# Chunk attention scores with 128 contraction rows, first weights in quarters, and a longer schedule search in a two-layer hybrid encoder

## The chip, the cores and the metric

The kernel runs on one core of a Trainium2 chip. The metric is the device time of one execution in microseconds; several executions give a median. A profiled execution also gives a trace of every instruction of the core's engines: TensorE (PE; its weight loads are shown apart as PEld), VectorE (DVE), ScalarE (ACT), GpSimd (POOL), and SyncE (SP), which here only issues DMAs.

## What is computed

The input is x of 512 tokens by 1024 channels, all in float32. Each of two layers applies an RMS norm and one input projection, whose columns feed three groups of attention heads; the heads' outputs are normalised, concatenated and projected back into x. Then come a second norm and a gated feed-forward part with a causal convolution of width 3. A last norm closes the program. Cut to its outline:

```python
for l in range(2):
    proj = rms_norm(x, attn_norm[l]) @ w_in[l]
    h_mla, h_diff, h_ch = split(proj)
    o_mla  = rms_norm(mla_attention(h_mla, ...))      # 6 heads, latent q and kv, rotary key
    o_diff = diff_attention(h_diff, ...)              # 6 heads, two softmaxes each
    o_ch   = rms_norm(chunk_attention(h_ch, bias))    # 4 heads of 64, the scores of this change
    x = x + concat(o_mla, o_diff, o_ch) @ w_out[l]
    x = x + conv_ffn(rms_norm(x, ffn_norm[l]), ...)   # silu(g) * u, width 2816
return rms_norm(x, final_norm)
# chunk attention, per head: softmax(q @ k.T / 8 + bias[clip(i - j)]) @ v,
# chunks of 64 tokens, causal by chunk
```

## The kernel before

**Tiles and precision.** Activations lie transposed: 128 channels on the partitions, 512 tokens along the free axis. So x is eight tiles of 128x512. A weight block is 128x128 and the moving operand 128x512. TensorE multiplies fp32r numbers, which keep only the upper part of an fp32 number. To keep precision every operand is split in two: hi, the number cast to fp32r, and lo, what is left (`split`, L581: a cast on ACT or DVE, then a subtraction on DVE, called a low here). A product is three matmuls into one PSUM bank, hi·hi, hi·lo and lo·hi (`mm3` L576, `proj` L768). A projection of 1024 channels to 128 columns is thus 24 matmuls of 512 columns, and nearly all of TensorE's time is such matmuls.

**Weights.** They stream in once, 512 KB for a unit of 128 columns, through SP's queue (`weights`, L539). `halves` (L555) makes their hi and lo; for most the lo is a negated hi to which a DMA of POOL's queue adds the raw weights. The first three units (kv, q0, q1 of layer 0) come in two half DMAs each, cast and subtracted on DVE, while x lands in eight DMAs (`load_inputs`, L610).

**Stages of a layer.** `ORDER` (L81) lists the units: latent projections (kv, q0, q1, kr), the values (v, e, g), expansions of the latents (u), q and k of the differential heads (d) and of the chunk heads (c), and the output weights (a, b). A unit waits for its weights, for a PSUM bank (three for projections, two for scores, two for transposes and sums, one for products) and for its gate. Beside the units run two streams: `scores` (L1270) goes through the heads in the order latent, differential, chunk, each in four blocks of 128, 256, 384 and 512 keys (`softmax_rows`, L787: matmuls, then a reduction on DVE, then an exponential on ACT); `products` (L1294) transposes the probabilities and multiplies them with the values. Scores of the latent heads contract 128 rows, and those of the differential heads 96, which `stack` (L1092) gathers by DMAs of POOL's queue.

**Chunk heads.** `chunk_qk` (L936) makes two units, q and k of two heads at once: a tile of 128 partitions holds head 2u in rows 0 to 63 and head 2u+1 in rows 64 to 127, each with hi and lo. `chunk_head` (L1069) takes one head's 64 rows, and `three` (L808) gives three matmuls a block:

```python
return [(qt[r0 : r0 + n, a, :], kt[r0 : r0 + n, b, :]) for a, b in ((0, 0), (0, 1), (1, 0))]
```

**Latent values.** `latent_values` (L1015) projects the normalised latent to values in four blocks of 384 columns; DVE evicts each from its PSUM bank with the normalisation as factor.

**Second norm.** Each time an output projection is added to a tile of x, `gain_f.add` splits the tile for the feed-forward part and adds its square to a running sum; in `run_b` (L1144) that add runs on POOL.

**The order of instructions.** Every call of an engine is recorded (`Engine.call`, L357) with an estimated cost and its dependences, not issued; so in the trace nearly all instructions carry the line L364. When the whole program is recorded, `Clock.emit` (L335) orders it by a list schedule, backward and forward in turn, `ROUNDS` (L76) times, and keeps the one whose last start is earliest. Then everything is issued in that order, so the order on each engine is fixed ahead of the run and an instruction waits for all before it on its engine.

Of the kernel before, what the change touches and what calls it, by code (L numbers as in the profile page):

```python
# [52 lines left out]
for u in range(2):  # L53
    RINGS_R[f"cq{u}"], RINGS_R[f"ck{u}"] = ([RINGS_R["kmla"][2 * u + n]] for n in range(2))
    RINGS_R[f"vc{u}"] = [v[1 + u]]
for n in range(6):
# [3 lines left out]
for t, w, n in (("wraw", 1024, 2), ("P", GCOLS, 2), ("P1", GCOLS, 1), ("ev", S, 2), ("rb", S, 1), ("me", S, 1), ("acc", S, 1),  # L60
                ("y", S, 1), ("s", S, 1), ("o", S, 6), ("ol", S, 1)):
    RINGS_F[t] = (w, list(range(NF, NF + w * n, w)))
    NF += w * n
p0, o0, ol0 = (RINGS_F[t][1] for t in ("P", "o", "ol"))
RINGS_F["oc"], RINGS_F["om"], RINGS_F["od"] = (S, o0[0:2]), (S, o0[0:3]), (S, o0[3:6])
RINGS_F["ol"], RINGS_F["rbias"] = (S, [o0[5], ol0[0], o0[4]]), (S, [o0[2], ol0[0]])
# [8 lines left out]
NEVER = 1e9  # L75
ROUNDS = 4  # L76
TABLES = {AF.Exp: 1, AF.Ln: 1, AF.Sin: 2, AF.Silu: 3}
OUT = (1, 4, 7)
LATE = dict(qk=0, qm=0.5, og=0, lat=0, po=-99, hp=0, hs=99, sc=-0.2, p1=-0.5, st=-1, w=4)

ORDER = "kv q0 q1 kr e0 v e1 u0 u1 u2 d0 d1 d2 e2 c0 c1 g0 g1 a0 a1 a2 a3 a4 a5 a6 a7 b0 b1"  # L81

# [6 lines left out]
OA_FROM = 6  # L89
AHEAD = 1  # L90
NB_OUT = 1 << (8 // KB).bit_length() - 1

# [28 lines left out]
class Clock:  # L121
# [213 lines left out]
    def emit(self):  # L335


        start = self.list_schedule(list(range(len(self.ops))), lambda o: o.needs, lambda o: o.users, True)
        best = start
        for _ in range(ROUNDS):  # L340
            back = self.list_schedule([-(start[o.n] + o.cost) for o in self.ops], lambda o: o.users, lambda o: o.needs, False)
            start = self.list_schedule([-(back[o.n] + o.cost) for o in self.ops], lambda o: o.needs, lambda o: o.users, True)
            best = min(best, start, key=max)
        for o in sorted(self.ops, key=lambda o: (best[o.n], o.n)):
            o.emit()
# [134 lines left out]
def encoder(ctx, tc, xT, pos_row, pos_col, wflat, small, lam, relx, cst, out):  # L480
# [58 lines left out]
    def weights(l, name, run, finish, gate=lambda: True):  # L539
        o, c = offs[l, name]  # L540
        runs = [(0, c // 2), (c // 2, c)] if l == 0 and len(work.jobs) < 3 else [(0, c)]

        def part(raw, a, b):
            sp.dma_start(raw[:, a:b], wflat[o : o + P * c].rearrange("(p c) -> p c", p=P)[:, a:b])

        def fetch():
            raw = T("wraw")
            part(raw, *runs[0])
            if work.jobs[0].raw is None:
                rest_of_first.append(lambda: part(raw, *runs[1]))  # L550
            elif len(runs) > 1:
                part(raw, *runs[1])
            return raw
# [27 lines left out]
    def split(src, hi, lo):  # L581
# [6 lines left out]
        dve.tensor_tensor(lo, src, hi.bitcast(F32), op=ALU.subtract)  # L588


    widths = [KD * S, GCOLS, S, L * NCOL, cst.shape[1], P, NB, NB, 1]
# [18 lines left out]
    def load_inputs():  # L610

        work.jobs[0].fetch()
        sp.dma_start(sm[0], small[0])
        for k in range(KD):
            sp.dma_start(xs[k], xT[:, k, :])
            if k == 0:
                rest_of_first.pop()()
            if k == 1:
                work.jobs[1].fetch()
        sp.dma_start(posk_i, bass.AP(tensor=pos_row.tensor, offset=0, ap=[[0, P], [1, S]]))  # L620
        sp.dma_start(ct, cst)
        sp.dma_start(posq_i, pos_col)
# [185 lines left out]
    def three(qt, kt, r0, n):  # L808

        return [(qt[r0 : r0 + n, a, :], kt[r0 : r0 + n, b, :]) for a, b in ((0, 0), (0, 1), (1, 0))]  # L810
# [72 lines left out]
    def layer(l, gain_a):  # L883
# [51 lines left out]

        def chunk_qk(u):  # L936
            gate = lambda: (1, 1, 1) in stacks if u else ("m", 2, 1) in scored
            return [qk_unit(f"cq_{u}", f"cq{u}", gate, imm=CH_SCALE), qk_unit(f"ck_{u}", f"ck{u}", gate)]

# [129 lines left out]
        def chunk_head(h, qt, kt, buf, res):  # L1069
            rbias = biases[h]  # L1070
            yield from softmax_rows(three(qt, kt, 64 * (h % 2), 64), lambda i: rbias[:, S - 128 * (i + 1) :], -1.0, res, buf)
            scaled(*res)
            if h + 2 < CH_H:
                biases.append(load_bias(h + 2))
# [69 lines left out]
        def run_b(t, w):  # L1144
            for n in range(NB_OUT):
                c = slice(128 * KB * n, 128 * KB * (n + 1))
                acc = yield from proj(og[KA:], (w[0][:, c], w[1][:, c]), [])
                add_to_x(NB_OUT * t + n, acc)
                gain_f.add(NB_OUT * t + n, pool)

        jobs = {}

        def job(name):
            kind, t = name[0], int(name[1:]) if name[1:].isdigit() else 0
            return {
                "c": lambda: chunk_qk(t),
                "d": lambda: diff_qk(t),
# [93 lines left out]
        if l == 0:  # L1251
            load_inputs()
            exp_tables()
            work.jobs[0].load()
            for k in range(KD):
                gain_a.split(k)
                if k in (1, 4):
                    work.jobs[1 + k // 4].load()
            gain_a.squares()
            setup_rope()  # L1260
# [9 lines left out]
        def scores():  # L1270
            for n, (kind, u, j) in enumerate(heads):

                over = max((k + 1 for k in range(n) if bufs[k] in bufs[n] + "X" * (kind == "d")), default=0)
                need = [jobs[f"u{u}"]] if kind == "m" else jobs[f"{kind}{u}"][:2]
                yield lambda: 0.0 if all(b.done for b in need) and (kind != "d" or (u, j, 0) in stacks) and tailed[0] >= over else NEVER
# [251 lines left out]
```

## Time and profile before

| | before |
|---|---|
| device time, 3 runs | 1240.38, 1240.6, 1242.81 us; median 1240.6 |
| profiled execution | 1241.23 us, its span 1239.1 us |
| granted TensorE clock, mean | 0.995 |
| PE, PEld, DVE, ACT, POOL busy | 98%, 80%, 69%, 57%, 10% |
| moved by DMA | 146.33 MB, mean 118 GB/s |

Busy time is a share of the span, over stages that differ. The program's stages lie in time as follows: the start to about 15 us; the attention of layer 0 to about 240; its output projection and feed-forward part to about 640; then the same for layer 1, and the last norm at the end. A timeline lists instructions by start; consecutive like ones are one row with their count, and a bracket at the end gives the engine's idle time just before and what ended it. Ends of matmuls are modelled; their starts are recorded.

### The profile page before, as it was taken

The page shows a single profiled execution, that of the slowest core. Times are in us where ns is not written, and L with a number is a line of the kernel's source. Part 1 is how long each engine was busy: PE and PEld are TensorE (multiplying, and loading weights), DVE is VectorE, ACT ScalarE, POOL GpSimd, SP SyncE. Part 2 cuts the span into 40 slices and gives each one's busy share as a digit, 9 for nine tenths or more (in the row PEclk, how much of TensorE's full clock was granted, in tenths as well). Part 3 has the DMA queues.
Part 4 walks back from the last instruction along what each step waited for, and adds up shares of the span by engine and source line. Part 5 has one row for each costly group of instructions (what it writes and reads, how often), then busy time and mean ns, then how long its engine had stood idle before and what let it go on. Part 6 is the DMA issues. An engine that isn't in the chain of part 4 may idle for free.

```text
span 1239.1 us, 15626 instructions
## 1 busy us (share of the span) xinstructions
PE 1215.1 (98%) x5607; PEld 991.1 (80%) x5607; DVE 861.0 (69%) x1596; ACT 704.2 (57%) x1233; POOL 123.0 (10%) x181
## 2 busy tenths in 40 slices
PE   8999999999999999999999999999999999999996
PEld 5788887788888888888877888777888888888885
DVE  7798997588774357665457889976876633677643
ACT  6797996765443234444477899876544422444432
POOL 0214310130000000000011143003100000000000
PEclk9999999999999999999999999999999999999998
DMA  5848961733322332323477498436333233332232
GB/s 169 188 104 186 227 134 43 166 103 122 102 87 82 104 105 100 102 81 91 127 163 163 100 235 175 93 79 151 103 102 102 77 97 116 102 96 91 79 97 79
DMA packets 51613, 146.33 MB, mean 118 GB/s; under 512 B 6480, under 2 KB 9552, under 8 KB 51536
## 3 DMA queue, kind: packets, MB, share of 16 engines
q1 hardware_dynamic: 37280, 106.27, 28.1%
q0 software_dynamic: 14256, 39.07, 17.5%
q8 instruction: 44, 0.72, 0.2%
q14 instruction: 33, 0.27, 0.1%
HBM read 132.21 MB, written 2.10 MB: 108 GB/s over the span
## 4 chain that ended last, share of the span: by engine, by line
PE 92%; DVE 3%; ACT 2%; DMA 2%; issue 1%; SPq 0%; DVEq 0%; ACTq 0%; POOLq 0%
PE psproj L364 80%; PE pss L364 5%; PE pspt L364 4%; PE psav L364 3%; DVE af L364 1%; DVE ar L364 1%; DMA ar<-in_wflat 1%; ACT ar L364 1%; ACT af L364 1%; DVE xa L364 1%; DMA xa<-in_xT 1%; DMA af<-in_wflat 0%; SPq L364 0%; ACT L880 0%; ACT rope L364 0%
## 5 line engine op out<-in xcount | busy, mean ns | idle before, releaser
L364 PE MATMUL psproj<-ar 128*128 128x512 f32 (+1 forms) x4595 | 1104.7, 392 | 8.3 <-DVE xa L364 2.2
L364 PEld LDWEIGHTS psproj<-ar 128*128 128x128 f32 x4595 | 849.3, 188 | 184.7 <-DVE ar L364 4.7
L364 ACT CAST ar<-af 128x512 fp32r<-128x512 f32 (+4 forms) x333 | 268.4, 820 | 219.8 <-PE psproj L364 195.7
L364 DVE TENSOR_TENSOR ar<-af,ar 128x512 fp32r<-128x512 f32 (+4 forms) x260 | 239.7, 925 | 145.3 <-PE psproj L364 79.3
L364 DVE SCALAR_TENSOR_TENSOR af<-af,sma 128x511 f32<-128x511 f32 (+1 forms) x192 | 141.9, 748 | 7.5 <-ACT af L364 4.9
L364 ACT ACTIVATE af<-af,sma 128x512 f32<-128x512 f32 x88 | 71.3, 816 | 121.2 <-DVE af L364 121.2
L364 DVE TENSOR_TENSOR af<-psproj,af 128x512 f32<-128x512 f32 x108 | 73.6, 686 | 61.4 <-PE psproj L364 61.0
L364 POOL DMA_DIRECT2D ar<-in_wflat x61 | 54.0, 886 | 617.8 <-ACT ar L364 601.0
L364 ACT ACTIVATE af<-af 128x512 f32<-128x512 f32 (+1 forms) x106 | 65.4, 622 | 71.6 <-DVE af L364 71.0
L364 ACT ACTIVATE af<-af,mn 128x128 f32<-128x128 f32 (+3 forms) x176 | 98.2, 559 | 7.4 <-DVE mn L364 7.0
L364 PE MATMUL pss<-ar 128*128 128x128 f32 (+7 forms) x336 | 88.1, 333 | 0.6 <-DVE mn L364 0.4
L364 PEld LDWEIGHTS pss<-ar 128*128 128x128 f32 (+2 forms) x336 | 56.6, 187 | 19.4 <-issue 7.7
L364 DVE TENSOR_TENSOR xa<-xa,psproj 128x512 f32<-128x512 f32 (+1 forms) x65 | 43.5, 674 | 40.4 <-PE psproj L364 40.3
L364 DVE TENSOR_TENSOR af<-af 128x512 f32<-128x512 f32 (+2 forms) x71 | 48.0, 677 | 33.4 <-ACT af L364 33.0
L364 DVE TENSOR_TENSOR ar<-pspt,ar 128x512 fp32r<-128x512 f32 (+1 forms) x106 | 63.2, 603 | 6.3 <-ACT ar L364 3.5
L364 PE MATMUL psav<-ar 128*128 128x512 f32 (+3 forms) x256 | 64.9, 331 | 0.3 <-DVE af L364 0.2
L364 PE MATMUL pspt<-ident,af 128*128 128x128 f32 x360 | 63.3, 275 | 0.3 <-DVE af L364 0.3
L364 ACT ACTIVATE ar<-af 128x1024 fp32r<-128x1024 f32 (+3 forms) x61 | 58.0, 950 | 8.0 <-PE psproj L364 5.6
L364 PEld LDWEIGHTS pspt<-ident,af 128*128 128x128 f32 x360 | 45.2, 140 | 14.4 <-DVE af L364 2.3
L364 PEld LDWEIGHTS psav<-ar 128*128 128x128 f32 x256 | 44.6, 189 | 8.8 <-issue 1.3
L364 ACT CAST ar<-pspt 128x512 fp32r<-128x512 f32 (+1 forms) x73 | 37.6, 524 | 17.1 <-PE pspt L364 15.5
L364 DVE CUSTOM_DVE_ANT_0 af<-pss,dist 128x384 f32<-128x384 f32 (+2 forms) x96 | 45.3, 484 | 2.9 <-PE pss L364 2.8
(67 smaller groups left out, 564.2 us busy)
## 6 DMA issues: line engine op xcount, KB each, us to landing
af<-in_wflat SPq DMA_DIRECT2D x125, 512.0 KB, 3.5
ar<-in_wflat POOLq DMA_DIRECT2D x37, 512.0 KB, 8.0
af<-in_wflat SPq DMA_DIRECT2D x48, 384.0 KB, 3.0
af<-in_wflat SPq DMA_DIRECT2D x38, 320.0 KB, 2.9
ar<-ar POOLq DMA_DIRECT2D x72, 128.0 KB, 6.2
ar<-in_wflat POOLq DMA_DIRECT2D x16, 384.0 KB, 6.2
xa<-in_xT SPq DMA_DIRECT2D x8, 256.0 KB, 6.8
af<-in_wflat SPq DMA_DIRECT2D x8, 256.0 KB, 3.8
```

The costliest lines, as they stand in the source:

```text
L364: self.clock.issue(self.name, op, outs, ins + aps, func, lambda: fn(*args, **kw))
```

## The change

Four things change. **First, the chunk scores.** `chunk_qk` becomes two units. `chunk_q` makes one tile for each of the two heads, whose own 64 rows hold the hi and whose other 64 rows hold the lo. `chunk_k` makes two tiles for each head (hi and lo), splits them in the head's own rows, and a DMA of POOL's queue copies them (64 partitions, 256 KB) to the other rows. A block of scores is then two matmuls of 128 rows: [q hi; q lo] by [k hi; k hi], and the same by [k lo; k lo]. The product lo·lo, formerly left out, is now included. The unit of k gets a later gate and a place of its own in `ORDER`. **Second, the first three weights** are fetched in quarters, in turn with the tiles of x, and cast and subtracted by quarters. **Third, the schedule**: 60 rounds, with a disturbance of the ranks in each (normal, deviation 0.5 us), compared by their end, and started again from the best when a round falls behind it by more than 0.3 us. **Fourth, the squares** in `run_b` are added on DVE.

```diff
+    RINGS_R[f"cy{u}"] = [RINGS_R["x"][u]]
...
+RINGS_F["wfirst"] = (2 * S, o0[0:1])
...
-ROUNDS = 4
+ROUNDS = 60
...
-ORDER = "kv q0 q1 kr e0 v e1 u0 u1 u2 d0 d1 d2 e2 c0 c1 g0 g1 a0 ... b0 b1"
+ORDER = "kv q0 q1 kr e0 v e1 u0 u1 u2 d0 d1 d2 e2 c0 y0 c1 y1 g0 g1 a0 ... b0 b1"
...
+FIRST = 4
...
     def emit(self):
-        start = self.list_schedule(list(range(len(self.ops))), lambda o: o.needs, lambda o: o.users, True)
-        best = start
+        forth = lambda rank: self.list_schedule(rank, lambda o: o.needs, lambda o: o.users, True)
+        back = lambda rank: self.list_schedule(rank, lambda o: o.users, lambda o: o.needs, False)
+        span = lambda start: max(t + o.cost for t, o in zip(start, self.ops))
+        rnd = random.Random(0)
+        best = start = forth([o.n for o in self.ops])
         for _ in range(ROUNDS):
-            back = self.list_schedule([-(start[o.n] + o.cost) for o in self.ops], lambda o: o.users, lambda o: o.needs, False)
-            start = self.list_schedule([-(back[o.n] + o.cost) for o in self.ops], lambda o: o.needs, lambda o: o.users, True)
-            best = min(best, start, key=max)
+            late = back([rnd.gauss(0, 0.5) - start[o.n] - o.cost for o in self.ops])
+            start = forth([-(late[o.n] + o.cost) for o in self.ops])
+            best = min(best, start, key=span)
+            if span(start) > span(best) + 0.3:
+                start = best
...
     def weights(l, name, run, finish, gate=lambda: True):
-        runs = [(0, c // 2), (c // 2, c)] if l == 0 and len(work.jobs) < 3 else [(0, c)]
+        first = l == 0 and len(work.jobs) < 3
+        step = c // FIRST if first else c
+        runs = [(a, a + step) for a in range(0, c, step)]
...
     def load_inputs():
-        work.jobs[0].fetch()
+        for n in range(3):
+            work.jobs[n].fetch()
         sp.dma_start(sm[0], small[0])
         for k in range(KD):
             sp.dma_start(xs[k], xT[:, k, :])
-            if k == 0:
-                rest_of_first.pop()()
-            if k == 1:
-                work.jobs[1].fetch()
+            if k % (KD // FIRST) == 0:
+                for parts in rest_of_first:
+                    parts.pop(0)()
...
-        def chunk_qk(u):
-            gate = lambda: (1, 1, 1) in stacks if u else ("m", 2, 1) in scored
-            return [qk_unit(f"cq_{u}", f"cq{u}", gate, imm=CH_SCALE), qk_unit(f"ck_{u}", f"ck{u}", gate)]
+        def chunk_q(u):
+            def finish(job, acc, rb):
+                f = tmp("ev")
+                dve.scalar_tensor_tensor(f, acc, CH_SCALE, rb, op0=ALU.mult, op1=ALU.mult)
+                t = pair(f"cq{u}")
+                for j in range(2):
+                    own, other = slice(64 * j, 64 * j + 64), slice(64 - 64 * j, 128 - 64 * j)
+                    high(f[own, :], t[own, j, :])
+                    dve.tensor_tensor(t[other, j, :], f[own, :], t[own, j, :].bitcast(F32), op=ALU.subtract)
+                job.set(t)
+            return unit(f"cq_{u}", gain_a, finish, lambda: (1, 1, 1) in stacks if u else ("m", 2, 1) in scored)
+
+        def chunk_k(u):
+            def finish(job, acc, rb):
+                f = tmp("ev")
+                dve.tensor_tensor(f, acc, rb, op=ALU.mult)
+                ks = [pair(f"ck{u}"), pair(f"cy{u}")]
+                for j, t in enumerate(ks):
+                    own, other = slice(64 * j, 64 * j + 64), slice(64 - 64 * j, 128 - 64 * j)
+                    high(f[own, :], t[own, 0, :])
+                    dve.tensor_tensor(t[own, 1, :], f[own, :], t[own, 0, :].bitcast(F32), op=ALU.subtract)
+                    pool.dma_start(t[other, :, :], t[own, :, :])
+                job.set(ks)
+            return unit(f"ck_{u}", gain_a, finish, lambda: (2, 1, 1) in stacks)
...
         def chunk_head(h, qt, kt, buf, res):
-            yield from softmax_rows(three(qt, kt, 64 * (h % 2), 64), lambda i: rbias[:, S - 128 * (i + 1) :], -1.0, res, buf)
+            yield from softmax_rows([(qt[:, h % 2, :], kt[h % 2][:, n, :]) for n in range(2)], lambda i: rbias[:, S - 128 * (i + 1) :], -1.0, res, buf)
...
-                gain_f.add(NB_OUT * t + n, pool)
+                gain_f.add(NB_OUT * t + n)
```

`high` is the cast half of `split`, on ACT or DVE.

Three places show what this does to the order. TensorE, the first chunk head of layer 0 (pss are score banks, psproj projections, pspt transposes and sums, psav products; the blocks of 128, 256 and 384 keys), before:

```order
L364 MATMUL psproj_1_64<-ar_61 128x512 x5
L364 MATMUL pss_0_66<-ar_61 128x128 x3
L364 MATMUL psproj_1_64<-ar_61 128x512 x3
L364 MATMUL psproj_2_65<-ar_61 128x512 x2
L364 MATMUL pss_1_67<-ar_61 128x256 x3
L364 MATMUL psproj_2_65<-ar_61 128x512 x4
L364 MATMUL pspt_0_68<-ident_76,af_62 128x128
L364 MATMUL pss_0_66<-ar_61 128x384 x3
```

and after the change:

```order
L375 MATMUL pss_0_66<-ar_61 128x128 x2
L375 MATMUL pspt_1_69<-ident_76,af_62 128x128 x2
L375 MATMUL psproj_1_64<-ar_61 128x512 x2
L375 MATMUL pspt_0_68<-ar_61,bones_81 128x512
L375 MATMUL psproj_1_64<-ar_61 128x512 x4
L375 MATMUL pss_1_67<-ar_61 128x256 x2
L375 MATMUL psproj_1_64<-ar_61 128x512 x8
L375 MATMUL psav_0_70<-ar_61 128x384 x2
L375 MATMUL pss_0_66<-ar_61 128x384 x2
```

Each block has two matmuls in place of three, and the rows between them are shorter pieces of other work.

VectorE, the latent values of layer 1 (the 128x3x2x64 operations evict a bank of them; the scalar_tensor_tensor after pspt and the one after it finish the norm of a latent q), before:

```order
L364 TENSOR_TENSOR af_62<-psproj_1_64,af_62 128x512
L364 SCALAR_TENSOR_TENSOR af_62<-pspt_0_68,af_62 128x512
L364 SCALAR_TENSOR_TENSOR af_62<-af_62 128x512
L364 TENSOR_TENSOR ar_61<-pspt_1_69,ar_61 128x8x64
L364 TENSOR_TENSOR ar_61<-psproj_2_65,ar_61 128x3x2x64
L364 TENSOR_TENSOR ar_61<-psproj_0_63,ar_61 128x3x2x64
L364 SCALAR_TENSOR_TENSOR af_62<-af_62,sma_74 128x512 x2
L364 TENSOR_TENSOR ar_61<-psproj_1_64,ar_61 128x3x2x64
```

and after the change:

```order
L375 TENSOR_TENSOR af_62<-psproj_1_64,af_62 128x512
L375 TENSOR_TENSOR ar_61<-psproj_0_63,ar_61 128x3x2x64
L375 TENSOR_TENSOR ar_61<-psproj_2_65,ar_61 128x3x2x64
L375 TENSOR_TENSOR ar_61<-psproj_1_64,ar_61 128x3x2x64
L375 SCALAR_TENSOR_TENSOR af_62<-pspt_0_68,af_62 128x512
L375 TENSOR_TENSOR ar_61<-pspt_1_69,ar_61 128x8x64
L375 SCALAR_TENSOR_TENSOR af_62<-af_62 128x512
L375 SCALAR_TENSOR_TENSOR af_62<-af_62,sma_74 128x512 x2
L375 TENSOR_TENSOR ar_61<-psproj_2_65,ar_61 128x3x2x64
```

Three evictions now stand ahead of the scalar_tensor_tensor that reads pspt, where they stood behind the one after it or further down.

POOL, from the chunk units to the feed-forward part of layer 0 (128x1024 and 128x768 from in_wflat are weight accumulations, the 64x1024 from ar to ar the copies of k, the TENSOR_TENSOR the squares), before:

```order
L364 MEMSET af_62 64x64
L364 DMA ar_61<-in_wflat 128x1024
L364 DMA ar_61<-in_wflat 128x768
L364 MEMSET af_62 128x512
L364 MEMSET af_62 64x64
L364 DMA ar_61<-in_wflat 128x768 x2
L364 MEMSET af_62 64x64 x2
L364 DMA ar_61<-in_wflat 128x768 x5
L364 DMA ar_61<-in_wflat 128x1024 x2
L364 TENSOR_TENSOR af_62<-af_62 128x512 x7
```

and after the change:

```order
L375 DMA ar_61<-in_wflat 128x1024 x2
L375 DMA ar_61<-ar_61 64x1024
L375 DMA ar_61<-in_wflat 128x1024
L375 DMA ar_61<-ar_61 64x1024
L375 DMA ar_61<-in_wflat 128x768 x2
L375 DMA ar_61<-ar_61 64x1024 x2
L375 DMA ar_61<-in_wflat 128x768
L375 MEMSET af_62 64x64
L375 MEMSET af_62 128x512
L375 MEMSET af_62 64x64 x2
L375 DMA ar_61<-in_wflat 128x768 x5
L375 DMA ar_61<-in_wflat 128x1024 x6
```

The seven adds are gone, and four copies stand between the weight accumulations.

## Rows read from the trace of the kernel before

**Rows 1.** First lines of the page: span; busy us, share, count by engine.

```profile
span 1239.1 us, 15626 instructions
...
PE 1215.1 (98%) x5607; PEld 991.1 (80%) x5607; DVE 861.0 (69%) x1596; ACT 704.2 (57%) x1233; POOL 123.0 (10%) x181
```

**Rows 2.** Windows: length, busy us of PE, PEld, DVE, ACT, POOL (count), clock, DMA share, GB/s.

```profile
400.00:625.00 225.00, 225.00 (x994) 186.25 (x993) 126.67 (x165) 90.18 (x116) 2.61 (x3) 1.00 0.35 104
120.00:140.00 20.00, 20.00 (x104) 16.62 (x103) 19.98 (x62) 19.62 (x46) 8.98 (x15) 1.00 1.14 247
180.00:200.00 20.00, 20.00 (x101) 14.44 (x100) 16.46 (x51) 13.36 (x34) 1.00 (x2) 1.00 0.37 89
200.00:220.00 20.00, 20.00 (x94) 13.74 (x92) 15.89 (x43) 15.56 (x37) 1.01 (x2) 1.00 0.11 32
780.00:800.00 20.00, 20.00 (x102) 15.22 (x102) 18.27 (x53) 17.09 (x42) 2.59 (x3) 1.00 0.61 127
```

**Rows 3.** Timeline of PE, a chunk head: start, us, engine, operation, count, idle before.

```profile
200.72 1.07 PE L364 MATMUL psproj<-ar 128*128 128x512 f32 x4
201.72 0.96 PE L364 MATMUL pss<-ar 64*128 64x512 f32 x3
202.61 0.50 PE L364 MATMUL psav<-ar 128*128 128x512 f32 x1
202.94 0.62 PE L364 MATMUL psproj<-ar 128*128 128x512 f32 x2
```

**Rows 4.** Timeline of PE, score blocks of 128 rows.

```profile
665.02 0.68 PE L364 MATMUL psproj<-ar 128*128 128x512 f32 x2
665.54 0.52 PE L364 MATMUL pss<-ar 128*128 128x256 f32 x3
665.90 1.31 PE L364 MATMUL psproj<-ar 128*128 128x512 f32 x5
```

**Rows 5.** Groups by form, weight loads of scores: busy, mean ns, idle before and its end.

```profile
L364 PEld LDWEIGHTS pss<-ar 96*128 96x128 f32 x96 | 18.0, 188 | 4.0 <-DVE mn L364 0.4
...
L364 PEld LDWEIGHTS pss<-ar 64*128 64x128 f32 x96 | 14.3, 185 | 10.2 <-issue 7.3 <-DVE ar L364 1.0 <-DVE rl L364 0.4
```

**Rows 6.** Groups by form, casts and lows of 64 rows.

```profile
L364 DVE TENSOR_TENSOR ar<-psproj,ar 64x512 fp32r<-64x512 f32 x12 | 8.2, 687 | 4.2 <-ACT ar L364 3.9
...
L364 ACT CAST ar<-psproj 64x512 fp32r<-64x512 f32 x12 | 7.0, 581 | 2.8 <-PE psproj L364 2.4 <-DVE ar L364 0.2
```

**Rows 7.** DMA issues: count, KB each, median us to landing.

```profile
ar<-ar POOLq DMA_DIRECT2D x6, 256.0 KB, 7.3
```

**Rows 8.** Timeline of PE, latent values of layer 1.

```profile
647.77 1.31 PE L364 MATMUL psproj<-ar 128*128 128x384 f32 x6 [0.75 <-DMA ar<-in_wflat]
651.28 1.76 PE L364 MATMUL psproj<-ar 128*128 128x384 f32 x4 [2.20 <-DVE ar L364]
```

**Rows 9.** Timeline of DVE, the same stretch.

```profile
648.74 0.69 DVE L364 SCALAR_TENSOR_TENSOR af<-pspt,af 128x512 f32<-128x512 f32 x1 [2.62 <-ACT af L364]
...
650.68 1.01 DVE L364 TENSOR_TENSOR ar<-psproj,ar 128x384 fp32r<-128x384 f32 x2
```

**Rows 10.** Windows, the stretch behind that wait.

```profile
651.00:654.40 3.40, 3.12 (x8) 2.74 (x9) 3.28 (x7) 2.07 (x5) 0.87 (x1) 0.50 0.67 170
```

**Rows 11.** Groups by form, adds on POOL.

```profile
L364 POOL TENSOR_TENSOR af<-af 128x512 f32<-128x512 f32 x14 | 22.3, 1596 | 16.7 <-ACT af L364 15.8
```

**Rows 12.** Timeline of DVE, second norm of layer 1.

```profile
857.33 0.75 DVE L364 SCALAR_TENSOR_TENSOR ar<-xa,sma,ar 128x512 fp32r<-128x512 f32 x1
...
858.59 4.57 DVE L364 SCALAR_TENSOR_TENSOR ar<-xa,sma,ar 128x512 fp32r<-128x512 f32 x3
```

**Rows 13.** Timeline of PE, the same stretch.

```profile
863.81 4.42 PE L364 MATMUL psproj<-ar 128*128 128x512 f32 x18 [2.21 <-DVE xa L364]
```

**Rows 14.** Timeline of SP, the start.

```profile
3.08 1.38 SPq L364 DMA_DIRECT2D xa<-in_xT  x3
```

**Rows 15.** Timeline of PE, the start.

```profile
9.12 0.80 PE L364 MATMUL psproj<-ar 128*128 128x512 f32 x1 [1.68 <-ACT ar L364]
```

More of the change, by code (lines that the diff above doesn't have):

```diff
@@ L2 @@
 import math
+import random
 from contextlib import ExitStack
@@ L79 @@
 LATE = dict(qk=0, qm=0.5, og=0, lat=0, po=-99, hp=0, hs=99, sc=-0.2, p1=-0.5, st=-1, w=4)
-ORDER = "kv q0 q1 kr e0 v e1 u0 u1 u2 d0 d1 d2 e2 c0 c1 g0 g1 a0 a1 a2 a3 a4 a5 a6 a7 b0 b1"
+ORDER = "kv q0 q1 kr e0 v e1 u0 u1 u2 d0 d1 d2 e2 c0 y0 c1 y1 g0 g1 a0 a1 a2 a3 a4 a5 a6 a7 b0 b1"
 HEADS = "m0 m1 m2 d0 d1 d2 c0 c1"
@@ L540, in weights @@
         o, c = offs[l, name]
-        runs = [(0, c // 2), (c // 2, c)] if l == 0 and len(work.jobs) < 3 else [(0, c)]
+        first = l == 0 and len(work.jobs) < 3
+        step = c // FIRST if first else c
+        runs = [(a, a + step) for a in range(0, c, step)]
+        ring = "wfirst" if first and len(work.jobs) == 2 else "wraw"
         def part(raw, a, b):
@@ L546, in fetch @@
         def fetch():
[L547 to L552, printed above, removed]
+            raw = T(ring)
+            if first:
+                rest_of_first.append([lambda a=a, b=b: part(raw, a, b) for a, b in runs])
+            else:
+                part(raw, 0, c)
             return raw
@@ L588, in split, with high @@
         dve.tensor_tensor(lo, src, hi.bitcast(F32), op=ALU.subtract)
+    def high(src, hi):
+        n = hi.ap[-1][1]
+        if clock.through("act", 0.1 + n / 1200, src) < clock.through("dve", 0.07 + n / 1920, src) + LATE["hs"]:
+            act.copy(hi, src)
+        else:
+            dve.tensor_copy(hi, src)
     widths = [KD * S, GCOLS, S, L * NCOL, cst.shape[1], P, NB, NB, 1]
@@ L1155, in job @@
             return {
-                "c": lambda: chunk_qk(t),
+                "c": lambda: chunk_q(t),
+                "y": lambda: chunk_k(t),
                 "d": lambda: diff_qk(t),
@@ L1253, in layer @@
             exp_tables()
-            work.jobs[0].load()
+            for n in range(3):
+                work.jobs[n].load()
             for k in range(KD):
                 gain_a.split(k)
-                if k in (1, 4):
-                    work.jobs[1 + k // 4].load()
             gain_a.squares()
@@ L1273, in scores @@
                 over = max((k + 1 for k in range(n) if bufs[k] in bufs[n] + "X" * (kind == "d")), default=0)
-                need = [jobs[f"u{u}"]] if kind == "m" else jobs[f"{kind}{u}"][:2]
+                need = [jobs[f"u{u}"]] if kind == "m" else jobs[f"d{u}"][:2] if kind == "d" else [jobs[f"c{u}"], jobs[f"y{u}"]]
                 yield lambda: 0.0 if all(b.done for b in need) and (kind != "d" or (u, j, 0) in stacks) and tailed[0] >= over else NEVER
```

## The prediction

> **What bounds the kernel now.** I read the page's first lines first: TensorE is busy 1215.1 of 1239.1 us [rows 1], so a part of the change is worth what it takes from or adds to TensorE's own row of matmuls. The profiled execution took 1241.23 us, 2.13 more than its span; the median of the three runs is 1240.6, 0.6 less. All sums below are made against 1241.23, and 0.6 comes off at the end.
>
> Then I asked by stretch what else is full. In the feed-forward stretch 400 to 625 TensorE does 994 matmuls in 225.00 us, 0.226 each, with VectorE at 56%: nothing but the count of matmuls matters there. In 120 to 140, where softmax rows, new q and k tiles and the products overlap, VectorE is busy 19.98 and ScalarE 19.62 of 20 us: there they bound it as much as TensorE. In the stretches of the chunk heads, 180 to 220 and from 780, VectorE is at 79 to 91% and TensorE shows full, yet does 101, 94 and 102 matmuls per 20 us with many short ones among them [rows 2].
>
> What the fullness hides is in TensorE's timeline of a chunk head. Four projection matmuls of 512 columns start at 200.72 and the next group at 201.72: 1.00 us for four, against 4 x 0.226 = 0.91. The three 64-row score matmuls last 0.89 until the next starts, against 0.68. The product after them takes 0.33 until 202.94, against 0.226 [rows 3]. So one block loses 0.09 + 0.21 + 0.10 = 0.40 us, on the way in, between the 64-row ones and on the way out. Blocks of 128 rows show nothing of this: two projections in 0.52, three scores of 256 columns in 0.36, that is 0.12 each [rows 4]. The weight loader says the same over the whole program: it idled 10.2 us before its 96 loads of 64 rows and 4.0 before the 96 loads of 96 rows [rows 5].
>
> **The change part by part.**
>
> *Chunk scores of 128 rows, fewer matmuls.* Four heads, four blocks and two layers give 32 blocks, and each has two matmuls where it had three. With 512 columns a matmul costs 0.226 [rows 2], with 256 it costs 0.12 [rows 4]; the line through both gives 0.173 for 384 and 0.07 for 128, of which the shortest may cost as much as the 0.12, so I take 0.1. So 8 x (0.226 + 0.173 + 0.12 + 0.1) = 5.0 us go, all on the path. **-5.0.**
>
> *The switches to and from 64 rows.* The 32 blocks each lose about 0.37 (0.40 in the one shown; the shorter blocks that I looked at 0.31 to 0.38): 12 us. Some blocks are broken into pieces, as the order of instructions shows, and those switch more often, up to 15 us. The lower end is the loader's 10.2 - 4.0 = 6.2 [rows 5]. After the change every matmul of the program has 96 or 128 rows. I take 12, since a matmul's start is seen and the loader's idle time is only part of it. **-12 (-15 to -6.2).**
> Two pages of the Trainium skill bear on this. "TensorE: Matmul & The Clock Gate", in its part on what happens when you issue a matmul, says the time of a weight load goes with the columns and the row count doesn't matter; by it alone this term would be 0 and the sum 12 us higher. [Rows 3, 4] show otherwise. "TensorEngine Tiling (Array Packing)", under Key Properties, says that a change of tiling mode drains TensorE, which is what the 0.1 us at either edge look like.
>
> *What the new operands cost VectorE and ScalarE.* The q and k of a pair of heads were split in 128x512 operations; now each half is split apart. Counted from the order, VectorE gets 16 lows of 64x512 in place of 8 of 128x512, and the casts go from 8 of 128x512 to 16 of 64x512. A 64-row low takes 0.687 and a 64-row cast 0.581 [rows 6], so it is the columns that cost: per layer 4 x 0.687 = 2.75 us more for VectorE and 4 x 0.581 = 2.3 more for ScalarE or VectorE. In a stretch with slack that is nothing. But the chunk stretch 180 to 220 holds 16.46 + 15.89 = 32.35 us of VectorE in 40, and TensorE is to lose some 8.5 of the 40 [rows 2], so 31.5 us of TensorE would stand beside 35.1 of VectorE. If nothing moves, each layer gives 3.6 us back, 7.2 in all, about 8 with the casts. If the schedule spreads the lows into its neighbours, nothing. I take 3, nearer to nothing because VectorE has slack after 220 and the new order moves its work freely. **+3 (0 to +8).**
>
> *Key copies.* Each k unit sends two DMAs of 64 partitions through POOL's queue, 8 in the program. The copies of that size landed 7.3 us after issue [rows 7]. POOL itself is at 10% and its queue stands between weight accumulations, as the order shows. I cost them at nothing: what hides them are the matmuls of the units between a k projection and its first scores, seven microseconds of which are only some thirty matmuls. If that cover is missing they are rival C. **0.**
>
> *The search over the schedule.* I name the two waits that it visibly touches. In layer 1 TensorE waits 2.20 us at 651.28 for VectorE to empty a bank of the latent values [rows 8]; VectorE had run two scalar_tensor_tensor and an add from 648.74 before it came to these at 650.68 [rows 9]. The clock granted in 651.00 to 654.40 was 0.50, that is the 1.2 GHz level, after TensorE had stood still [rows 10]; 3.4 us at half speed cost another 1.7. The new order puts three of those evictions first. So up to 3.9; I take 3, because something of the wait may move to the next bank. The 0.75 us before 647.77 wait on a weight accumulation and stay. **-3 (-6 with like gaps elsewhere, to 0).**
>
> *Squares of the second norm on VectorE.* POOL's 14 adds take 1.596 us each, 22.3 in all [rows 11], and while three of them run from 857.58, three VectorE operations that took 0.75 us just before take 4.57 [rows 12]; then TensorE waits 2.21 us for VectorE's residual [rows 13]. On VectorE the adds should cost 0.69 each, by the like number of columns [rows 6], far less than what POOL's hold up there. So the 2.21 goes, but for what an add still delays: **-2 (-2.2 to 0).**
>
> *First weights in quarters.* SyncE issues twelve DMAs where it issued six, at 1.38 / 3 = 0.46 us each [rows 14], so the last tile of x is issued some us later, while TensorE, which waited 1.68 us at 9.12 [rows 15], has the columns of three weights to multiply with each tile that is there. The same bytes must land. I take a little of the wait: **-1 (-2.5 to +1).**
>
> *The tail.* The last two output halves are interleaved, which may put the last store one or two matmuls later: **+0.4 (0 to 1).**
>
> Sum: -5.0 - 12 + 3 + 0 - 3 - 2 - 1 + 0.4 = -19.6. 1241.23 - 19.6 = 1221.6, and 0.6 less for the median: **1221.0 us**. The forecast's own range is 1214 to 1226: terms don't all fall to one side.
>
> **The rivals.**
>
> *A, VectorE takes the bound over.* For it: 19.98 and 19.62 of 20 us at 120 to 140 and 18.27 at 780 to 800 [rows 2], and every added operation lies near these. Then the 8 us of the stretch come back, and the four lows that fall into full stretches cost another 2.75 per layer: 8 + 5.5 = 13.5 in place of 3, 1231; half of it, 1226. Against: 60 rounds of the search against 4, and free VectorE time right behind. Price 1226 to 1233, chance 0.16.
>
> *B, row count costs nothing and the gaps of [rows 3] have another cause,* such as a read of VectorE's or the trace's modelled ends. Then -12 falls away: 1233. Against: starts are not modelled, and the three edges show in every 64-row block I looked at and in none of 128 rows. The page named above would have it so. Chance 0.03.
>
> *C, slower: key copies on POOL's queue.* If TensorE has no other work while a k unit's copies fly, each of the four units (two per layer) stalls it by up to 7.3 us [rows 7], with a fall of the clock behind it, as at 651 where a 2.20 us wait cost another 1.7 [rows 8, 10]. Half uncovered, 4 x (3.65 + 1.7) = 21.4; wholly, 36. It decides from 19.6 / 4 = 4.9 us per unit on. Then 1242 to 1257, most likely near 1245. Against: the projections of v and of the output weights stand between, and the search counts this latency. Chance 0.05.
>
> *D, the search finds more.* TensorE was idle 24 us of the span [rows 1]; part of that is the start and the tail. If it takes another 8 to 16 us of short waits and low-clock stretches: 1205 to 1213. Chance 0.06. Against: the named waits are the longest, and the rest are of fractions of a us.
>
> **How the numbers follow.** Forecast 0.70, A 0.16, B 0.03, C 0.05, D 0.06. The range for 8 in 10 takes the forecast's bounds and those of A and reaches to 1212 for part of D: 1212 to 1233. A measurement of this kernel can tell some 0.2%, 2.5 us, from no change. Below 1238.1 lie the forecast, A, B and D, less a little for terms that all turn out small: 0.92. Within 0.2%: 0.03. Slower: 0.05, which is C.
>
> **What would show it.** Right: no group of 64 rows among the score matmuls, and blocks of two at the pitch of their columns; the stretches of the chunk heads some 8 us shorter in each layer; no 2.20 us wait at the latent values of layer 1 and full clock behind it; no POOL adds and no 2.21 us wait near 860. A is right if TensorE's idle time in the chunk stretches ends on VectorE and VectorE is above 95% there. C is right if score matmuls wait on the copies' DMA. B is right if the pitch of two 128-row scores is longer than their columns. I am wrong in size if the edges of the 64-row blocks were filled by something that is still there.

## The result and the profile after

The changed kernel takes 1221.01 us (median of 4, 1218.77 to 1222.27) against 1241.34 for the kernel before in the same session; the ratio is 0.9833, with a 95% interval of 0.9814 to 0.9852. The prediction was 1221.0. The profiled execution of the changed kernel took 1218.77 us with a span of 1217.0.

The first lines of its page, which answer to [rows 1]:

```profile
span 1217.0 us, 15607 instructions
...
PE 1198.0 (98%) x5575; PEld 984.0 (81%) x5575; DVE 859.4 (71%) x1628; ACT 709.6 (58%) x1243; POOL 104.6 (9%) x175
```

TensorE is as full as before, with 32 matmuls fewer. Its windows (columns as in [rows 2]):

```profile
400.00:625.00 225.00, 225.00 (x995) 186.37 (x994) 126.50 (x166) 93.46 (x124) 3.45 (x4) 1.00 0.34 103
...
180.00:200.00 20.00, 20.00 (x113) 16.53 (x112) 19.75 (x57) 18.30 (x45) 3.84 (x8) 1.00 0.64 134
200.00:220.00 20.00, 19.93 (x112) 16.35 (x112) 18.61 (x50) 16.93 (x37) 2.64 (x3) 1.00 0.45 96
780.00:800.00 20.00, 20.00 (x116) 17.06 (x115) 19.85 (x55) 17.92 (x45) 2.00 (x4) 1.00 0.48 114
```

The feed-forward stretch is unchanged. The windows of the chunk heads now hold 113, 112 and 116 matmuls where they held 101, 94 and 102, and VectorE went from 79 to 91% up to 93 to 99%. TensorE's timeline of a chunk head, which answers to [rows 3]:

```profile
190.08 0.63 PE L375 MATMUL psproj<-ar 128*128 128x512 f32 x2
190.55 0.62 PE L375 MATMUL psav<-ar 128*128 128x512 f32 x2
191.01 0.40 PE L375 MATMUL psproj<-ar 128*128 128x512 f32 x1
191.24 0.34 PE L375 MATMUL psav<-ar 128*128 128x384 f32 x1
191.42 0.62 PE L375 MATMUL pss<-ar 128*128 128x512 f32 x2
191.88 0.39 PE L375 MATMUL psproj<-ar 128*128 128x512 f32 x1
```

The block of 512 keys takes 191.88 - 191.42 = 0.46 us, twice 0.23, and nothing is lost on the way in or out. The latent values of layer 1, on TensorE and on VectorE ([rows 8, 9]):

```profile
638.69 0.28 PE L375 MATMUL pspt<-ident,af 128*128 128x128 f32 x1
638.72 6.74 PE L375 MATMUL psproj<-ar 128*128 128x512 f32 x29
```

```profile
636.75 1.02 DVE L375 TENSOR_TENSOR ar<-psproj,ar 128x384 fp32r<-128x384 f32 x2
638.66 0.56 DVE L375 TENSOR_TENSOR ar<-psproj,ar 128x384 fp32r<-128x384 f32 x1 [0.89 <-ACT ar L375]
639.19 0.69 DVE L375 SCALAR_TENSOR_TENSOR af<-pspt,af 128x512 f32<-128x512 f32 x1
```

Three banks are emptied ahead of the scalar_tensor_tensor, and TensorE waits for none: 29 matmuls in 6.74 us, 0.23 each, at a granted clock of 1.00 from 638 to 646. At the second norm of layer 1 ([rows 13]) TensorE shows no gap either. At the start ([rows 15]) the 1.68 us wait is gone, and one of 0.69 at 4.27 is left, which was 0.92:

```profile
4.27 2.08 PE L375 MATMUL pspt<-af,ones 128*128 128x512 f32 x2 [0.69 <-ACT af L375]
5.36 4.00 PE L375 MATMUL psproj<-ar 128*128 128x512 f32 x6
9.15 1.38 PE L375 MATMUL pspt<-af,ones 128*128 128x512 f32 x2
...
854.79 13.45 PE L375 MATMUL psproj<-ar 128*128 128x512 f32 x57
```

The key copies' queue, among the DMA issues ([rows 7]; the 14 are 8 key copies and the 6 of before):

```profile
ar<-ar POOLq DMA_DIRECT2D x14, 256.0 KB, 6.2
```

To see where the 22.1 us of span went I cut the program at three matmuls that all versions have: the last 96-row score of layer 0, the first score of layer 1 and the last 96-row score of layer 1, each by its start in TensorE's timeline. All stretches run from one start to the next, in one profiled execution of each kernel. The third stretch is nearly all attention without chunk scores, the second and fourth begin with the chunk heads.

| us | to last 96-row score, layer 0 | to first score, layer 1 | to last 96-row score, layer 1 | to the end |
|---|---|---|---|---|
| before | 181.41 | 482.44 | 122.34 | 452.87 |
| changed | 176.78 | 472.82 | 120.70 | 446.69 |
| chunk part alone (chunk_only) | 180.93 | 478.04 | 122.74 | 447.08 |
| changed, old ordering (no_search) | 178.08 | 476.21 | 122.93 | 444.43 |
| changed, lows twice (lows_twice) | 178.76 | 476.27 | 125.38 | 452.69 |

The change gains 4.6, 9.6, 1.6 and 6.2 us. The chunk part alone gains 0.5, 4.4, nothing and 5.8: it works where the chunk heads are. The second stretch holds the latent values too, whose wait is gone. More can't be read from these cuts: with another order, other matmuls move across a cut, so a gain in the first or third stretch has no shown cause.

### The profile page after: what moved, and what is told of

Its sections match the earlier page's. It is cut to its first block, busy times and chain, and to the rows that moved or that the text cites. A ratio compares the mean times of both kernels' runs of the same rounds, so it can differ in the third digit from the quotient of the medians.

```text
span 1217.0 us, 15607 instructions
## 1 busy us (share of the span) xinstructions
PE 1198.0 (98%) x5575; PEld 984.0 (81%) x5575; DVE 859.4 (71%) x1628; ACT 709.6 (58%) x1243; POOL 104.6 (9%) x175
## 3 DMA queue, kind: packets, MB, share of 16 engines
q0 software_dynamic: 14896, 41.17, 18.6%
## 5 line engine op out<-in xcount | busy, mean ns | idle before, releaser
L375 ACT CAST ar<-af 128x1024 fp32r<-128x1024 f32 (+4 forms) x341 | 273.4, 816 | 229.0 <-PE psproj L375 163.9
L375 DVE TENSOR_TENSOR ar<-af,ar 128x1024 fp32r<-128x1024 f32 (+5 forms) x274 | 242.9, 892 | 114.6 <-PE psproj L375 70.3
L375 DVE TENSOR_TENSOR af<-af 128x512 f32<-128x512 f32 (+2 forms) x85 | 57.7, 679 | 35.0 <-ACT af L375 33.9
L375 PE MATMUL pss<-ar 128*128 128x128 f32 (+7 forms) x304 | 79.8, 327 | 0.8 <-DVE mn L375 0.4
L375 PE MATMUL pspt<-ident,af 128*128 128x128 f32 x360 | 66.0, 275 | 1.3 <-DVE af L375 1.2
L375 PEld LDWEIGHTS pss<-ar 128*128 128x128 f32 (+1 forms) x304 | 53.3, 189 | 12.7 <-DVE mn L375 4.2
L375 POOL DMA_DIRECT2D ar<-ar x86 | 47.4, 590 | 63.5 <-DVE ar L375 18.4
```

What stands on the lines that cost most here:

```text
L375: self.clock.issue(self.name, op, outs, ins + aps, func, lambda: fn(*args, **kw))
```

## The experiments

The runs take the terms of the prediction apart and test its rivals B (row count costs nothing) and A (VectorE takes the bound over). Every ratio is to the kernel before on the same chip in the same session, whose median was 1241.45, 1241.04 and 1239.93 in the three sessions of four kernels each: rows_only to chunk_only, search_only to other_seed, and the last four.

One measure from the traces serves most of them. A chunk stretch is the time from the last 96-row score of a layer to its last chunk score, start to start. Its matmuls would need a certain time if each took the pitch at which 128-row matmuls start one behind the other (0.227, 0.174, 0.119 and 0.060 us for 512, 384, 256 and 128 columns, and 0.08 for a transpose, its mean). What the stretch takes more than that is its time beyond the columns. Differences between kernels are surer here than the figures themselves.

| | chunk stretch of layers 0 and 1, us | matmuls | beyond the columns, both layers, us |
|---|---|---|---|
| before | 38.42, 37.95 | 184, 183 | 19.7 |
| rows_only | 31.07, 31.16 | 184, 183 | 5.6 |
| third_dropped_64 | 34.71, 35.02 | 168, 167 | 17.7 |
| third_dropped_128 | 30.45, 30.20 | 168, 167 | 8.6 |
| chunk_only | 31.10, 31.29 | 176, 178 | 7.1 |
| search_only | 46.09, 38.92 | 201, 186 | 24.3 |
| no_chunk | 36.25, 37.70 | 178, 173 | 20.2 |
| rows_and_search | 34.71, 31.74 | 201, 186 | 5.7 |
| changed | 30.16, 32.19 | 166, 184 | 5.7 |
| lows_twice | 34.36, 32.77 | 153, 162 | 17.0 |

### Rows alone: rows_only

```diff
-            yield from softmax_rows(three(qt, kt, 64 * (h % 2), 64), ...
+            yield from softmax_rows(three(qt, kt, 0, 128), ...
```

> The kernel before with one argument changed: the three score matmuls of a chunk block contract all 128 rows of the tiles (both heads of the pair) instead of one head's 64. It computes the sum of two heads' scores in place of each head's own. Count of matmuls, columns, operands, copies and the order on every engine stay as before. Theory (a switch to and from 64 rows costs about 0.37 us a block, 32 blocks): 12 us faster, 1229 (1226 to 1235). Rival B (row count costs nothing): 1241, no change.

Measured: 1227.91 us, ratio 0.9889 (0.9869 to 0.9909). The order on TensorE, VectorE and ScalarE is row for row that of before; only the rows contracted differ (the kernel computes the sum of two heads' scores). So 13.5 us lay in the switches, and rival B falls. The two chunk stretches, with the same matmuls, are 14.1 us shorter together. Weight loads by form, which answer to [rows 5], and a block in TensorE's timeline:

```profile
L364 PEld LDWEIGHTS pss<-ar 128*128 128x128 f32 x240 | 40.3, 189 | 7.3 <-DVE mn L364 0.8 <-DVE ar L364 0.6 <-issue 0.5
L364 PEld LDWEIGHTS pss<-ar 96*128 96x128 f32 x96 | 18.0, 188 | 4.0 <-DVE mn L364 0.4
```

```profile
197.62 0.85 PE L364 MATMUL pss<-ar 128*128 128x512 f32 x3
198.30 0.39 PE L364 MATMUL psav<-ar 128*128 128x512 f32 x1
198.53 0.61 PE L364 MATMUL psproj<-ar 128*128 128x512 f32 x2
```

The same 96 loads sat behind 10.2 us of idle loader; now all 240 together have 7.3, of which the other 144 had 5.2 before. The block lasts 0.68, three times 0.227, and the product after it 0.23, against 0.89 and 0.33. The Trainium skill, in "TensorE: Matmul & The Clock Gate" (what happens when you issue a matmul), says row count doesn't matter for a weight load. The loads last 185 and 189 ns, which agrees; but what a load of 64 rows between others holds up is not in that sentence. The Trainium skill, in "TensorEngine Tiling (Array Packing)", Key Properties, says that a change of tiling mode drains TensorE. That would fit; whether these matmuls change the mode, no run here shows.

### Count alone, at 64 and at 128 rows: third_dropped_64 and third_dropped_128

```diff
-                pe.matmul(sc[:, :w], lhsT=q[:, qs], rhs=k[:, :w], start=m == 0, stop=m == len(pairs) - 1)
+                last = m == (1 if chunk else len(pairs) - 1)
+                pe.matmul(sc[:, :w], lhsT=q[:, qs], rhs=k[:, :w], start=m == 0, stop=last)
+                if chunk and m == 2:
+                    clock.ops[-1].emit = lambda: None
```

> The kernel before, scheduled with three 64-row matmuls a chunk block, of which the third (lo by hi) is left out when the program is issued; the order of everything else stays. It leaves out one of the three parts of the chunk scores. Theory: the columns of 32 matmuls, 5.0 us, and one of the inner edges of 0.1 us in each block, 3.2 us: 1233. Rival B: 5.0 us alone, 1236.

Measured: 1236.58, ratio 0.9959 (0.9945 to 0.9972): 4.9 us, the columns and nothing for the edge, so the theory's 1233 was missed. Rival B's number came out, though B had fallen with rows_only. The starts in the trace of the kernel before say why: of a group of 64-row matmuls the first takes 0.10 us beyond its columns and the last 0.09, but one between them 0.01 (medians of 29, 29 and 27). Leaving out one of three takes no edge away.

> Both edits above together: two matmuls of 128 rows a chunk block in the order of before, with the old operands (scores of the pair of heads, one part left out). Theory: 12 + 5.0 us off, 1224. Rival B: 5.0 off, 1236.

Measured: 1228.13, ratio 0.9883 (0.9858 to 0.9909): not told apart from rows_only, although 32 matmuls are gone. This missed by 4 us, which is about what the two intervals leave open. The table shows where columns went: the chunk stretches hold 4.6 us of columns less than in rows_only and are 1.6 us shorter. Windows and TensorE's timeline show what took the rest:

```profile
180.00:200.00 20.00, 19.94 (x113) 16.13 (x112) 19.62 (x60) 16.32 (x42) 1.00 (x2) 1.00 0.31 74
200.00:220.00 20.00, 19.21 (x106) 15.18 (x105) 17.55 (x47) 18.00 (x39) 2.72 (x4) 1.00 0.40 90
```

```profile
206.51 0.73 PE L364 MATMUL psav<-ar 128*128 128x512 f32 x2 [0.52 <-DVE af L364]
```

VectorE is busy 19.62 of 20 us at 180 to 200, and TensorE has idle time right behind. In the two chunk stretches every matmul that starts over 0.12 us later than its pitch had last waited for VectorE by the trace, 2.4 us in all; rows_only has none. With the switches gone, the old order leaves TensorE no room to run ahead there.

### The chunk part alone: chunk_only

The edit is the chunk part of the diff ahead of the prediction, put into the kernel before.

> The kernel before with the first part of the change alone: the new chunk q and k units with their key copies and two matmuls of 128 rows; halves of the first weights, 4 plain rounds, squares on POOL as before. Theory: -17 and +3 for the added lows and casts: 1227 (1224 to 1233). Rival A (VectorE takes the bound over): 13.5 back, about 1238. Rival C (copies late): over 1242.

Measured: 1230.61, ratio 0.9911 (0.9889 to 0.9933). That is 2.5 more than third_dropped_128, which has the same matmul shapes without the new lows, casts and copies; the prediction's +3 stood for this. The intervals overlap and the orders differ, so the size fits but isn't shown. Two windows in and behind its chunk stretches:

```profile
200.00:220.00 20.00, 18.66 (x104) 15.15 (x103) 18.66 (x55) 18.58 (x43) 1.85 (x3) 1.00 0.38 86
800.00:820.00 20.00, 18.42 (x103) 15.03 (x102) 18.88 (x51) 18.49 (x42) 1.91 (x3) 1.00 0.39 84
```

TensorE now idles 1.3 and 1.6 us in stretches where it was full, with VectorE and ScalarE both at 92% or more.

### The search alone, and all but the search: search_only and no_search

```diff
-ROUNDS = 4
+ROUNDS = 60
```

with the new `emit` put into the kernel before; the other kernel has the old `emit` and 4 rounds in the changed one.

> The kernel before with the new ordering alone (60 disturbed rounds, compared by their end); old chunk units, halves, squares on POOL. If the search is worth its own term whatever the chunk heads are: -3 (0 to -6), 1238. If it is worth most where VectorE is full, and the old chunk stretch was bound by 64-row switches which no order removes: -1 to -3, 1239.

Measured: 1241.68, ratio 1.001 (0.9997 to 1.0022), no gain; both figures of the expectation were missed. The wait at the latent values is gone there too (TensorE's longest wait for VectorE's ar is 0.3 us; one of 1.25 for ACT stands nearby, at 647.30), but the new order cuts the 64-row scores into 52 groups instead of 40, counted in the trace, and each group has both edges: 24.3 us beyond the columns against 19.7. One block of 512 keys in three pieces, in TensorE's timeline:

```profile
185.40 0.50 PE L370 MATMUL pss<-ar 64*128 64x512 f32 x1
185.83 0.55 PE L370 MATMUL pspt<-ident,af 128*128 128x128 f32 x3
186.13 0.36 PE L370 MATMUL psav<-ar 128*128 128x256 f32 x1
186.43 0.50 PE L370 MATMUL pss<-ar 64*128 64x512 f32 x1
186.86 0.33 PE L370 MATMUL pspt<-ident,af 128*128 128x128 f32 x1
187.12 0.49 PE L370 MATMUL pss<-ar 64*128 64x512 f32 x1
187.54 0.39 PE L370 MATMUL psav<-ar 128*128 128x256 f32 x1
```

Each 512-column score takes 0.42 to 0.43 us until the next start, against 0.226. The planner's costs know nothing of rows, so it mixes freely. A new wait of 2.0 us (products on ACT's ar) came on top; rows_and_search has it as well:

```profile
PE psav L370 <- ACT ar L370: 2.0, 1, 2.0
```

> The changed kernel with the old ordering (4 plain rounds). If the search is worth its own term: 1221 + 3 = 1224. If the new chunk stretch is bound by VectorE and the search is what spreads VectorE's work out of it: the chunk part alone gave 1230.6, less 2.2 for the squares and 1 for the quarters, so about 1227.

Measured: 1224.18, ratio 0.9872 (0.9849 to 0.9895), 3.2 above the changed kernel; the two intervals overlap. The wait at the latent values is there in full, which ties its end to the search. TensorE's timeline:

```profile
641.10 8.99 PE L370 MATMUL psproj<-ar 128*128 128x384 f32 x32 [2.12 <-DVE ar L370]
```

### All but the chunk part, and another seed: no_chunk and other_seed

no_chunk has the old `chunk_qk` and `three` in the changed kernel; other_seed has `random.Random(1)`.

> The changed kernel with the old chunk units and scores (three matmuls of 64 rows). If the parts add: 1241.4 - 3 - 2 - 1 + 0.4 = 1236. If search and chunk scores need each other: 1237 to 1239. Rival B (rows cost nothing) would have it at 1226.

Measured: 1235.40, ratio 0.9959 (0.9944 to 0.9974): the forecast of 1236 within a us, and the chunk part is worth 14 in the changed kernel by the medians (16 by the ratios), against 10.8 alone. But search_only, with the same search and no squares or quarters, was 6.3 slower. Most of that need not be the squares and quarters: the order found here has 40 groups of 64-row matmuls and not 52, and loses 4.1 us less beyond the columns in the chunk stretches.

> The changed kernel with another seed of the disturbance, nothing else. It shows how much of the time is the luck of one order. Expected 1221 to 1224; a rival that the search is mostly luck: 1227 or more.

Measured: 1221.67, ratio 0.9849 (0.9829 to 0.9869): with one other seed the time is the same, so it hardly hangs on one order.

### Rows and search together: rows_and_search

The edit of rows_only and the new `emit`, nothing else.

> Three 128-row matmuls a chunk block (the pair of heads summed, as in rows_only) and the new ordering of 60 rounds; all else as before. The search alone gave no change on the kernel before, whose 64-row scores it broke into 52 groups instead of 40. Theory (what the search won there went into the edges of 64-row groups): without such edges it is worth its own term, rows_only's 1227.9 less 3 to 5, 1223 to 1225. Rival (the search is worth nothing by itself): 1228.

Measured: 1221.53, ratio 0.9854 (0.9839 to 0.9868), faster than the 1223 to 1225 expected. The search, worth nothing on 64-row scores, is worth 0.35% of the time, some 4 us, without them, by the two ratios 0.9889 and 0.9854. And this kernel, with three matmuls a block, no key copies, no added lows, halves and POOL's adds, is as fast as the whole change within the intervals, which leave some 3 us either way. So fewer matmuls, quarters and squares on one side and the new operands on the other nearly cancel.

It also makes a second test of the switches. Its order is that of search_only, row for row on every engine, and only the rows contracted differ. The ratios 1.001 and 0.9854 make that worth some 19 us here, against 13.5 in the old order. The chunk stretches are 18.6 us shorter for 52 groups, against 14.1 for 40: 0.36 and 0.35 us a group. The 4.4 us between the two are as much as the search wins here, some 4, and explain why it won nothing alone.

### VectorE's cost doubled: lows_twice

```diff
                     dve.tensor_tensor(t[other, j, :], f[own, :], t[own, j, :].bitcast(F32), op=ALU.subtract)
+                    dve.tensor_tensor(t[other, j, :], f[own, :], t[own, j, :].bitcast(F32), op=ALU.subtract)
```

and the same for k.

> The changed kernel with each of the 64x512 lows of the chunk units done twice: 16 more VectorE operations, 8 in each layer, 0.687 each, 5.5 us a layer. If VectorE sets the pace around the new chunk stage: 5 to 11 us slower, 1226 to 1232. If the schedule can still spread it: 1221 to 1223.

Measured: 1233.00, ratio 0.9935 (0.9910 to 0.9959), 1% or some 12 us above the changed kernel, a us more than expected, for 16 x 0.687 = 11.0 us of VectorE. In the profiled execution, the slowest of the four, the chunk stretches lose 17.0 us beyond the columns against 5.7, so about all of it is on the path. Whether it acts as VectorE's pace or as a longer chain to the scores is not separated:

```profile
180.00:200.00 20.00, 17.16 (x80) 13.02 (x80) 19.77 (x51) 13.72 (x33) 2.15 (x4) 0.86 0.41 89
200.00:220.00 20.00, 18.99 (x100) 15.41 (x99) 18.65 (x51) 18.69 (x44) 2.84 (x5) 0.97 0.25 64
```

TensorE's timeline has waits such as the one below. After several of them the granted clock fell, 0.86 on average at 180 to 200: from 199.56 on projection matmuls start 0.43 us apart, at the 1.2 GHz level, so the waits cost more than their length. The order differs from the changed kernel's too, and a new wait of 2.3 us, for a weight accumulation, stands behind the chunk scores at 841.68.

```profile
189.55 0.55 PE L375 MATMUL pspt<-ident,af 128*128 128x128 f32 x3 [0.59 <-DVE af L375]
```

### Squares and quarters undone: pool_adds and halves

pool_adds puts `pool` back into `gain_f.add`; halves puts back `weights`, `load_inputs` and the first loads of before.

> The changed kernel with the squares in the b units of the output projection added on POOL again. The 2.21 us wait returns: 1223 (1221 to 1223.5).

Measured: 1221.37, ratio 0.9855 (0.9840 to 0.9871): not told apart from the changed kernel, whose interval ends at 0.9852. The 2.21 us wait did not return, as had been expected: the adds are on POOL, yet TensorE goes through the second norm of layer 1 without a gap.

```profile
847.83 5.69 POOL L375 TENSOR_TENSOR af<-af 128x512 f32<-128x512 f32 x3 [0.60 <-ACT af L375]
```

```profile
834.66 21.08 PE L375 MATMUL psproj<-ar 128*128 128x512 f32 x92
```

So in the new order the squares' move is not what ends that wait; in search_only, with POOL's adds as well, 0.6 us of it are left. In the old order (no_search) it is gone with the adds on DVE.

> The changed kernel with the first weights in halves, fetched and split as before. The quarters were costed at -1 (-2.5 to +1): 1222 (1220 to 1223.5).

Measured: 1222.44, ratio 0.9857 (0.9841 to 0.9873): the same. The 1.68 us wait at the start did not return either; the longest there, but for that of the first matmul, is 0.92. Both have orders of their own from the search, so the term of each is not isolated here. Together, in the old ordering, they are the step from chunk_only (0.9911) to no_search (0.9872): 0.4%, some 5 us, with intervals of 0.4% about each. By the first table, from single profiled executions, 2.9 lie before the last 96-row score of layer 0 and 2.7 behind that of layer 1, the stretches that hold the quarters and the squares of layer 1.

## Why the prediction was right, point by point

**The switches, -12:** right in mechanism and nearly in size; rows_only gave 13.5. The inner edges were misread: the cost goes by group of 64-row matmuls, 0.35 us each, whatever its length. So it grows with every block that an order breaks up, as the prediction said, but further, to some 19 us in search_only's order. The chunk stretches are 8.3 and 5.8 us shorter in the changed kernel, where 8 was forecast for each; other matmuls lie in them now.

**Fewer matmuls, -5.0, "all on the path":** this step failed as a term of its own. Dropping them after the rows were 128 gave nothing that can be told from noise (1228.13 against 1227.91), since TensorE then waited for VectorE. They were on the path only as long as the switches kept TensorE slower than VectorE: third_dropped_64 gave the 4.9. In the changed kernel no run isolates them. The shortest block was also taken at 0.1 us where its matmuls start 0.06 apart, which makes the sum 4.6.

**New operands, +3:** the size fits chunk_only against third_dropped_128, 2.5. The reason given, that the new order spreads them, holds for the changed kernel: its chunk stretches lose 5.7 us beyond the columns, as rows_only's do with 5.6, and 7.1 in chunk_only. But that room is used up: in lows_twice doubled lows cost their whole length. Rival A's mechanism, VectorE taking the bound over, did occur in the old order, at a lower price than A's: some 5.0 + 2.5 = 7.5 us by the times, so the chunk part alone is worth 10.8, where the terms -5.0, -12 and +3 gave 14.

**Key copies, 0:** right. No wait of TensorE in the changed kernel is put down to them, and the copies of that size landed 6.2 us after issue. Of the kernels with key copies only halves shows a wait for a DMA from ar to ar, and that is before a 96-row score, so for a differential head's copy. Rival C did not occur.

```profile
707.67 0.47 PE L373 MATMUL pss<-ar 96*128 96x128 f32 x2 [1.40 <-DMA ar<-ar]
```

**The search, -3:** the size was right in the changed kernel (1224.18 against 1221.01, with intervals that overlap), and the wait that was named is gone; so is the 0.75 us wait on a weight accumulation that was to stay. But it is no term of its own: on the kernel before it is 0, because the new order pays in 64-row edges what it saves.

**Squares and quarters, -2 and -1:** about 5 together without the search, and not measurable one by one with it. The waits of 2.21 and 1.68 us are gone, as forecast, but with the search they stay away with the old squares and the old halves too, so the mechanism is not shown for the changed kernel. No run tests the tail's +0.4.

So the total came out to the us partly by luck. Alone, the chunk part is worth 10.8 and the other three 5.6 (1241.04 against 1235.40), 16.5 together, and the whole change 20.3, with 2 to 3 us of noise in each. The sum had 14 and 5.6, and added them. What made up for the 3 missing in the chunk part is what the parts are worth to each other, for which the sum has no term: the search gains some 4 us once the 64-row groups are gone, and the chunk part loses less to VectorE in the search's order. The first of these two is shown by search_only and rows_and_search; the times alone hardly tell 16.5 from 20.3. The range and the switches were earned; the last digit was luck.

## What to carry to other kernels

When TensorE shows full, divide its time by its columns stretch by stretch: a stretch that does fewer matmuls in the same time holds a cost that busy time hides, such as switches between 64-row and full matmuls. Test it by changing the shape alone with the same order on every engine. A scheduler that minimises waits can spend what it wins on a cost that its model lacks, so put the switch into the model or remove it first. And measure a part both alone and by leaving it out of the whole: here the chunk part is worth 10.8 us one way and 14 the other.

## What the runs showed of the hardware that was not expected

Here a group of 64-row matmuls among 128-row ones cost some 0.35 us, whether it held one or several: 14.1 us of chunk stretch for 40 groups and 18.6 for 52, each from two kernels that differ in nothing else. In the kernel before it shows as four times 0.1 us beyond the columns: 0.10 on the matmul ahead, 0.10 on the first of the group, 0.09 on the last, 0.11 on the matmul behind (medians); one that stands alone has 0.20. Groups of 96 rows show 0.01 or less at these places. Padding the contraction to 128 rows was worth 13.5 us over 32 blocks, with the same number of matmuls. A correct kernel might get there with q tiles whose other 64 rows are zero, three matmuls a block and the old k tile, without key copies and without added lows for k; it was not tried. What exactly TensorE does at such a switch stays open.
